# A bidirectional mLSTM and neighbourhood-attention layer: state products for both directions as three split products of 258 columns

## The chip, the cores and the metric

The kernel runs on one core of a Trainium2 chip. The metric is device time in microseconds (us) of one execution. TensorE appears in the profile as PE (its weight loads as PEld), VectorE as DVE, ScalarE as ACT, GpSimd as POOL; SP is the sync engine, which issues most of the DMAs. The queues by which an engine issues DMAs are shown as SPq, ACTq, POOLq.

## The reference, cut to what matters

One layer over 2048 tokens of 1024 features, all float32. After a conditioned RMSNorm one projection gives the inputs of two groups: neighbourhood attention (8 heads of 64 on a grid 32 x 64) and a bidirectional mLSTM (4 heads of 128). q and k of the mLSTM go through a convolution of 5 taps and SiLU. The outputs of both groups are gated, joined, projected and added to x, and a final RMSNorm follows. The part that the change touches is the state recurrence of the mLSTM, run forwards and backwards:

```python
def step(carry, inp):
    C, n, m = carry
    ...
    w = jnp.exp(a_c - m_new[..., None])
    C_new = decay[..., None, None] * C + jnp.einsum('bhs,bhse,bhsd->bhed', w, v_c, k_c)
    n_new = decay[..., None] * n + jnp.einsum('bhs,bhsd->bhd', w, k_c)
```

The kernel works in chunks of 128 tokens (NC = 16 chunks, MH = 4 heads) and holds C and n of a head in one tile of 128 x 129 by giving v a column of ones: the state's addition in a chunk is the product of k (128 tokens x 128 features) with v (128 tokens x 129) scaled by the row weights w of that direction.

## The kernel before, in words

**Projections.** The large products are split: an operand x becomes a high part, rounded to float32r by ACT, and a low part, x minus high, by DVE, and a product is hi*hi + hi*lo + lo*hi on TensorE. The token blocks (`tok_blocks`) and the convolution (`conv_blocks`) come first. In the convolution each group of 512 tokens of one feature tile is projected (24 products of 512 columns), evicted by ACT, run through five taps on DVE (L1032, L1034) and SiLU on ACT (L1036), and stored in `d_ck`, a scratch tensor in device memory that holds for each head and chunk everything that the mLSTM reads. For k, TensorE also turns the four chunks of the group (L1045), ACT copies them out with the scale KSCALE (L1047) and SP stores them as 128 columns of `d_ck`, in front of v.

**The mLSTM.** `phase1b` takes the heads in turn, each in two passes. `ml_pass1` goes through the 16 chunks from both ends to the middle (0, 15, 1, 14, ...). `load` (SP queue, seven buffers) brings k and v of a chunk, 257 columns; `weight` scales v for the directions that need it (DVE, L1263: direction 1 into a tile of its own, `wv`, four buffers, direction 0 in place); a step makes one float32 product per direction (L1283), and the state of the next chunk is either updated from the one before (`follow`, DVE, L1267) or put aside by an ACT copy (L1294), to be joined later: at the end of the pass DVE runs 14 further `follow`s. In the first two steps of a head (chunks 0 and 15) one direction has no next chunk and gets no product. `ml_pass2` then computes the outputs chunk by chunk; its first product with a state is px (L1344).

**Fillers.** Between the steps `pump` puts products of `nq_gen` (L1094: the projections of attention's q and k and of the gates, 24 products of 512 columns per tile) on TensorE, PUMP1 = 4.5 per step of the first pass. For each weight column pair the fillers need a split too: an ACT copy to high (L1065, L1067) and a DVE subtraction to low (L1066, L1068); their results are evicted by ACT and DVE.

**Order.** Up to attention a planner of the framework orders each engine's instructions by its own costs and by readiness, so that an instruction may come well ahead of its place in the text. The attention part of `phase2` runs in `manual_schedule`, in the order as written. Attention's softmax works on a ring of ten tiles of 128 x 512. Since the transposes read some columns past the used ones, all ten are cleared to zero before, by GpSimd (L1748), just ahead of the hand-ordered part. The first slot of that part makes two pairs of scores (L1587, four PSUM banks), with the softmax of the first pair (L1598 on DVE, L1599 on ACT) between.

Of the kernel before, what the change touches and what calls it, by code (L numbers as in the profile page):

```python
# [8 lines left out]
F32 = mybir.dt.float32  # L9
F32R = mybir.dt.float32r  # L10
AF = mybir.ActivationFunctionType
ALU = mybir.AluOpType
# [3 lines left out]
P = 128  # L16
# [9 lines left out]
MH = 4  # L26
# [32 lines left out]
class Kernel:  # L59
# [30 lines left out]
    def scratch(self):  # L90
        d = self.dram
        self.d_vna = d.tile([T, 512], F32, name="d_vna")
        self.d_ck = d.tile([MH, NC, P, 897], F32, name="d_ck")
        self.d_mneg = d.tile([P, CH], F32, name="d_mneg")
        self.d_zna = d.tile([16, P, 4, P], F32, name="d_zna")
        self.d_zml = d.tile([16, P, 4, P], F32, name="d_zml")
        self.d_qna = d.tile([2, 16, P, 2, 2, P], F32, name="d_qna")
        self.d_kna = d.tile([2, 512, T], F32, name="d_kna")
        self.d_mix = d.tile([16, P, 4, P], F32, name="d_mix")
        self.d_wo = d.tile([KT, P, D], F32, name="d_wo")  # L100
        self.d_fnw = d.tile([1, D], F32, name="d_fnw")
        self.d_gate = d.tile([1, D], F32, name="d_gate")
        self.d_rneg = d.tile([NH, 15, 31], F32, name="d_rneg")
        nks = [24, 32, 24]
        self.d_e = [d.tile([NH // 2, 16, 2, 15, nks[t]], F32, name=f"d_e{t}") for t in range(3)]
        nrs = [11, 15, 12]
        self.d_t = [[d.tile([NH // 2, P, 2, nrs[r] * nks[t]], F32, name=f"d_t{r}{t}") for t in range(3)] for r in range(3)]
# [588 lines left out]
    def vo_group(self, h, slot, g, first=None, brow=None, tops=(), stage=None):  # L696
        nc = self.nc
        st = self.stage_tile(f"stvo_{h}_{g}") if stage is None else stage
        nc.gpsimd.memset(st[:, :, 128:129], 1.0)
        brow = brow if brow is not None else self.brows[h % 2]  # L700
        width = 272 if h == 0 else 256
        for o in range(4):
            tt = 4 * g + o
            if first:
                ps = first[o]
            else:
                ps = tops[o] if o < len(tops) else self.pp.tile([P, GT], F32, tag="pp", name=f"pvo_{h}_{tt}")
                self.tok_tile(ps[:, :width], self.wslot[slot], tt, width)
            pair = st[:, o].rearrange("p (j c) -> p j c", j=2)[:, :, 0:128]
            self.evicted = nc.vector.tensor_add(pair, ps[:, 0:256].rearrange("p (j c) -> p j c", j=2), brow.rearrange("p (j c) -> p j c", j=2))  # L710
            if h == 0:
                nc.vector.tensor_add(self.gates[:, :, tt], ps[:, 256:272], self.bgate)
            next(self.chain, None)
            if o == 1:
                self.flush()
        nc.scalar.activation(st[:, :, 129:257], st[:, :, 129:257], AF.Sigmoid)
        dst = self.d_ck[h, 4 * g : 4 * g + 4, :, 128:385].rearrange("o p c -> p o c")
        if g == 0 and h < 3:
            (nc.scalar if h == 0 else nc.sync).dma_start(dst, st[:, :, 0:257])
        else:  # L720
            self.defer(lambda: nc.sync.dma_start(dst, st[:, :, 0:257]))
# [186 lines left out]
    def decays(self, pool):  # L908

        nc = self.nc  # L910
        mask = pool.tile([P, 2, CH], F32, name="mask")
        nc.gpsimd.memset(mask, 0.0)
        nc.gpsimd.affine_select(out=mask[:, 0, :], in_=mask[:, 0, :], pattern=[[1, CH]], compare_op=ALU.is_ge, fill=-BIG, base=0, channel_multiplier=-1)
        nc.gpsimd.affine_select(out=mask[:, 1, :], in_=mask[:, 1, :], pattern=[[-1, CH]], compare_op=ALU.is_ge, fill=-BIG, base=0, channel_multiplier=1)
        groups = [(h, gi, d) for h in range(MH) for gi in range(NG) for d in range(2)]
        tiles = {}

        def load(n):
            h, gi, d = groups[n]
            t = tiles[n] = self.dec_tile(pool, f"dec_{n}")  # L920
            r = d * 64 + h * NC + 4 * gi
            src = self.d_mneg[r : r + 4].rearrange("r t -> (r t)").unsqueeze(0)
            self.behind(nc.sync.dma_start(t, src.broadcast_to([P, 512])), self.mark)

        def masked(n):
            t = tiles[n].rearrange("p (c t) -> p c t", c=4)
            nc.gpsimd.tensor_tensor(t, t, mask[:, groups[n][2]].unsqueeze(1).broadcast_to([P, 4, CH]), ALU.add)  # L927

        def raised(n):
            h, gi, d = groups[n]  # L930
            t = tiles.pop(n).rearrange("p (c t) -> p c t", c=4)
            for o in range(4):
                c = 4 * gi + o
                nc.scalar.activation(t[:, o, :], t[:, o, :], AF.Exp, bias=self.cols["g"][:, d, h, c : c + 1])  # L934
            dst = self.d_ck[h, 4 * gi : 4 * gi + 4, :, 641 + d * CH : 641 + (d + 1) * CH].rearrange("c p t -> p c t")
            nc.scalar.dma_start(dst, t)

        for n in range(len(groups) + 3):
            for step, fn in ((3, raised), (2, masked), (0, load)):
                if 0 <= n - step < len(groups):  # L940
                    fn(n - step)
            yield
# [80 lines left out]
    def conv_group(self, pool, u, kind, ct, g):  # L1023
# [11 lines left out]
        yield  # L1035
        nc.scalar.activation(acc, acc, AF.Silu, bias=self.cb[:, cc : cc + 1])  # L1036
        j = 0 if kind == "q" else 1
        dst = self.d_ck[ct, 4 * g : 4 * g + 4, :, 385 + j * CH : 385 + (j + 1) * CH].rearrange("c p t -> p c t")
        nc.sync.dma_start(dst, acc.rearrange("p (c t) -> p c t", t=CH))
        yield  # L1040
        if kind == "q":
# [1 line left out]
        ps = self.tp.tile([P, GT], F32, tag="tp", name=f"kt_{ct}_{g}")  # L1043
        for o in range(4):
            nc.tensor.transpose(ps[:, o * P : (o + 1) * P], acc[:, o * CH : (o + 1) * CH], self.ident)  # L1045
        st = self.stage_tile(f"stk_{ct}_{g}")[:, :, 0:128]
        nc.scalar.activation(st, ps.rearrange("p (a q) -> p a q", a=4), AF.Copy, scale=KSCALE)  # L1047
        d2 = self.d_ck[ct, 4 * g : 4 * g + 4, :, 0:128].rearrange("o p c -> p o c")
        nc.sync.dma_start(d2, st)


    def nq_load(self, i, s):
# [193 lines left out]
    def ml_pass1(self, ml, h):  # L1246
# [3 lines left out]
        order = [k // 2 if k % 2 == 0 else NC - 1 - k // 2 for k in range(NC)]  # L1250

        def load(k):
            t = tiles[k] = ml.tile([P, 257], F32, tag="kv", bufs=7, name=f"kv_{h}_{order[k]}")
            nc.sync.dma_start(t, self.d_ck[h, order[k], :, 0:257])

        def weight(k):
            c = order[k]
            v = tiles[k][:, 128:257]
            sides[k] = {d: v for d in range(2) if 0 <= c + 1 - 2 * d < NC}
            if len(sides[k]) == 2:  # L1260
                sides[k][1] = ml.tile([P, 129], F32, tag="wv", bufs=4, name=f"wv_{h}_{c}")
            for d in sorted(sides[k], reverse=True):
                nc.vector.tensor_scalar(sides[k][d], v, self.cols["w"][:, d, h, c : c + 1], None, ALU.mult)  # L1263

        def follow(d, c, dc):
            n = c + 1 - 2 * d
# [8 lines left out]
        for k, c in enumerate(order):  # L1275
            if k + 4 < NC:
                load(k + 4)
            self.flush(2)
            self.close_step()
            dc = self.ms.tile([P, 2, 256], F32, tag="s1", bufs=3, name=f"dc_{h}_{c}")  # L1280
            kt = tiles.pop(k)[:, 0:128]
            for d, w in sorted(sides[k].items()):
                nc.tensor.matmul(dc[:, d, :129], kt, w, start=True, stop=True)  # L1283
            if k + 2 < NC:
                weight(k + 2)
            for d in sorted(sides.pop(k)):
                n = c + 1 - 2 * d
                self.st[d][n] = ml.tile([P, 129], F32, tag=f"st{d}_{n}", name=f"st_{h}_{d}_{n}")
                if k < 2:
                    nc.vector.tensor_copy(self.st[d][n], dc[:, d, :129])  # L1290
                elif d == k % 2:
                    follow(d, c, dc[:, d, :129])
                else:
                    nc.scalar.activation(self.st[d][n], dc[:, d, :129], AF.Copy)  # L1294
            self.low()
            self.pump(PUMP1)
            yield
# [9 lines left out]
    def ml_pass2(self, ml, h):  # L1307
# [3 lines left out]

        def load(c):
            t = ml.tile([P, 769], F32, tag="ck", bufs=4, name=f"ck_{h}_{c}")
            nc.sync.dma_start(t, self.d_ck[h, c, :, 128:897])
            vo[c] = t[:, 0:257]
            qk[c] = t[:, 257:513].rearrange("p (j t) -> p j t", j=2)
            mb[c] = t[:, 513:769].rearrange("p (d t) -> p d t", d=2)
# [143 lines left out]
    def phase2(self):  # L1461
# [282 lines left out]
        pO = self.pool(pss, "pO", bufs=1, space=PSUM)  # L1744
        ring = [few.tile([P, 512], F32, tag=tag, bufs=bufs, name=f"ring_{i}") for i, (tag, bufs) in enumerate((("hm", 2), ("hm", 2), ("zt", 2), ("zt", 2)))]
        ring += [p.tile([P, 512], F32, name=f"ring_{i}") for i in range(4, 10)]
        for t in ring[4:] + ring[:4]:
            nc.gpsimd.memset(t, 0.0)  # L1748
        order = itertools.cycle(ring)
        turn = lambda: next(order)  # L1750
        b1 = patches[1]
# [113 lines left out]
                self.owed = 0  # L1865

        with self.tc.manual_schedule():
            for m in range(len(patches) + 1):
                slot(m)
            while len(done) < len(patches):  # L1870
# [94 lines left out]
```

## Time and profile before

| | us |
|---|---|
| median of 3 runs | 1277.48 (1276.66 to 1277.92) |
| profiled execution, its own time | 1276.39 |
| its span | 1274.5 |
| PE busy | 1264.4 (99%) |
| DVE busy | 790.3 (62%) |
| ACT busy | 537.7 (42%) |
| POOL busy | 201.7 (16%) |

The span is from the first to the last instruction of the profiled execution. Times within it are in us from its start. The granted TensorE clock was at full speed (0.999 on the mean). Matmuls overlap: one that lasts 0.4 us may be followed 0.23 us later by the next, so busy PE says nothing of how dense its work is. The convolution lies from about 310 to 490 us, the four heads from 533 to 905 us, attention and the output from 915 us on.

### The profile page before, as it was taken

What the parts mean: (1) busy time and instruction counts of PE and PEld (TensorE: products, weight loads), DVE (VectorE), ACT (ScalarE), POOL (GpSimd) and SP (SyncE); (2) the same over time, 40 slices, a digit from 0 to 9 for tenths busy, and PEclk for the clock granted to TensorE, in tenths of its full rate; (3) what the DMA queues carried; (4) which work ended last, traced back from release to release, by engine and by line L of the source; (5) the groups of instructions that cost most, each with busy time, mean ns of one, the idle gap of its engine ahead of it and who ended that gap; (6) DMA issues with size and microseconds to landing.
All of it is one profiled execution on the core that took longest, in us unless ns stands there. A gap on an engine that the chain in (4) does not pass through costs nothing.

```text
span 1274.5 us, 22948 instructions
## 1 busy us (share of the span) xinstructions
PE 1264.4 (99%) x8168; PEld 1095.4 (86%) x8168; DVE 790.3 (62%) x2391; ACT 537.7 (42%) x1182; POOL 201.7 (16%) x368
## 2 busy tenths in 40 slices
PE   9999999999999999999999999999999999999997
PEld 8999999999888888888888888888877888888886
DVE  7875542213667664267777778777556766767664
ACT  6642425442334222123323323324357565565552
POOL 0000003440000000000001001000424331332541
PEclk9999999999999999999999999999999999999999
DMA  9999947996678764745757867746677755655551
GB/s 366 335 309 286 283 147 198 249 245 180 180 180 189 165 154 115 207 131 164 204 160 207 251 189 215 240 149 186 207 249 266 230 162 160 203 177 176 176 173 67
DMA packets 217082, 259.08 MB, mean 203 GB/s; under 512 B 23435, under 2 KB 163595, under 8 KB 216968
## 3 DMA queue, kind: packets, MB, share of 16 engines
q1 hardware_dynamic: 149542, 190.09, 52.1%
q0 software_dynamic: 13616, 37.28, 8.9%
q10 hardware_dynamic: 53810, 30.24, 8.4%
q8 instruction: 65, 1.06, 0.3%
q14 instruction: 49, 0.40, 0.1%
HBM read 173.05 MB, written 92.72 MB: 209 GB/s over the span
## 4 chain that ended last, share of the span: by engine, by line
PE 95%; DVE 2%; ACT 1%; issue 1%; DMA 0%; DVEq 0%; ACTq 0%
PE pq L1094 27%; PE y L1676 14%; PE pc L639 5%; PE pc L640 5%; PE pc L638 5%; PE pO L1633 4%; PE pT L1618 3%; PE pvo L638 3%; PE pvo L640 3%; PE pvo L639 3%; PE pS L1587 3%; PE pvo L693 3%; PE pv L640 2%; PE pv L639 2%; PE pv L638 2%; PE pi L1346 2%
## 5 line engine op out<-in xcount | busy, mean ns | idle before, releaser
L1094 PE MATMUL pq<-hhi,whi_a 128*128 128x512 f32 x512 | 208.4, 407 | 0.0
L1094 PE MATMUL pq<-hlo,whi_a 128*128 128x512 f32 x512 | 207.8, 406 | 0.0
L1094 PE MATMUL pq<-hhi,wlo_a 128*128 128x512 f32 x512 | 207.2, 405 | 0.0
L1368 POOL TENSOR_TENSOR hm<-hm,ck 128x128 f32<-128x128 f32 x64 | 28.2, 440 | 580.3 <-DVE hm L1367 541.0
L1094 PEld LDWEIGHTS pq<-hhi,wlo_a 128*128 128x128 f32 x512 | 96.8, 189 | 16.7 <-issue 0.2
L1094 PEld LDWEIGHTS pq<-hlo,whi_a 128*128 128x128 f32 x512 | 96.7, 189 | 16.1 <-issue 0.4
L1094 PEld LDWEIGHTS pq<-hhi,whi_a 128*128 128x128 f32 x512 | 96.8, 189 | 15.9
L1599 ACT ACTIVATE ring<-ring,mn 128x480 f32<-128x480 f32 (+5 forms) x128 | 75.9, 594 | 55.8 <-DVE mn L1598 55.8
L1620 ACT ACTIVATE ring<-pT 96x384 f32<-96x384 f32 (+3 forms) x128 | 65.8, 514 | 63.5 <-PE pT L1618 62.0
L1676 PE MATMUL y<-hhi,wlo_a 128*128 128x512 f32 (+1 forms) x272 | 87.0, 394 | 0.2 <-ACT y L1683 0.2
L1676 PE MATMUL y<-hhi,whi_a 128*128 128x512 f32 x256 | 86.2, 408 | 0.0
L1349 ACT ACTIVATE num<-px,gtile 128x129 f32<-128x129 f32 x120 | 38.7, 367 | 105.2 <-PE px L1344 91.5
L1522 POOL DMA_DIRECT2D v<-d_vna x158 | 78.7, 505 | 15.6 <-issue 4.4
L1618 PEld LDWEIGHTS pT<-ident,ring 128*128 128x128 f32 (+2 forms) x416 | 51.1, 136 | 19.2 <-ACT ring L1620 3.7
L1618 PE MATMUL pT<-ident,ring 128*128 128x128 f32 (+2 forms) x416 | 66.2, 272 | 0.0
L638 PE MATMUL pvo<-whi_b,hhi 128*128 128x256 f32 x224 | 63.6, 284 | 0.0
L1598 DVE CUSTOM_DVE_ANT_0 ring<-pS,tab 128x480 f32<-128x480 f32 (+5 forms) x128 | 61.9, 539 | 2.6 <-PE pS L1587 2.4
L640 PE MATMUL pvo<-whi_b,hlo 128*128 128x256 f32 x224 | 63.1, 282 | 0.0
L639 PE MATMUL pvo<-wlo_b,hhi 128*128 128x256 f32 x224 | 63.0, 281 | 0.0
L934 ACT ACTIVATE dec<-dec,gtile 128x128 f32<-128x128 f32 x128 | 41.3, 391 | 46.9 <-POOL dec L927 43.2
L673 DVE TENSOR_TENSOR stv<-pv,brow 128x256 f32<-128x256 f32 x32 | 13.6, 425 | 71.8 <-PE pv L640 71.8
L710 DVE TENSOR_TENSOR stvo<-pvo,brow 128x256 f32<-128x256 f32 x60 | 24.7, 418 | 50.7 <-PE pvo L640 40.0
(343 smaller groups left out, 3331.3 us busy)
## 6 DMA issues: line engine op xcount, KB each, us to landing
ck<-d_ck SPq DMA_DIRECT2D x64, 384.5 KB, 3.6
rawq<-in_w_main_dram SPq DMA_DIRECT2D x28, 512.0 KB, 5.2
raw<-in_w_main_dram SPq DMA_DIRECT2D x18, 512.0 KB, 6.2
kv<-d_ck SPq DMA_DIRECT2D x64, 128.5 KB, 3.0
dec<-d_mneg SPq DMA_DIRECT2D x32, 256.0 KB, 6.0
d_ck<-dec ACTq DMA_DIRECT2D x32, 256.0 KB, 6.9
qs<-d_qna SPq DMA_DIRECT2D x30, 256.0 KB, 3.9
xr<-in_x_p_dram POOLq DMA_DIRECT2D x15, 512.0 KB, 3.9
```

Of the source, the lines that this page charges most:

```text
L638: nc.tensor.matmul(ps, lhi(k), rhi(k), start=(k == 0), stop=False)
L639: nc.tensor.matmul(ps, lhi(k), rlo(k), start=False, stop=False)
L640: self.mark = nc.tensor.matmul(ps, llo(k), rhi(k), start=False, stop=(k == KT - 1))
L934: nc.scalar.activation(t[:, o, :], t[:, o, :], AF.Exp, bias=self.cols["g"][:, d, h, c : c + 1])
L1094: self.mark = nc.tensor.matmul(patch_ps(ps) if patch else ps, w, self.htok(h, g, k, patch), start=(k == 0 and n == 0), stop=(k == KT - 1 a ...
L1522: queue.dma_start(chunks[key][r * nkc : (r + 1) * nkc, :], rows[r])
L1598: nc.vector.tensor_tensor_reduce(pt[:, :nk], ps, tabs[ct][:, j * nk : (j + 1) * nk], 1.0, 3e38, ALU.add, ALU.min, mn)
L1599: nc.scalar.activation(pt[:, :nk], pt[:, :nk], AF.Exp, bias=mn, scale=-1.0, accum_out=sums[:, j : j + 1])
L1618: nc.tensor.transpose(ps[:cs, i, :], U[u][j][:, i * cs : (i + 1) * cs], self.ident)
L1620: nc.scalar.activation(t[:cs, :nch, :], ps[:cs, :nch, :], AF.Copy)
L1633: nc.tensor.matmul(po[j * HD : (j + 1) * HD, ct, :], v[:n, h * HD : (h + 1) * HD], pt[j][:n, i, :], start=(i == 0), stop=(i == nch - 1))
L1676: nc.tensor.matmul(y, m[:, k, :], w[k][:, cs], start=(k == 4 and n == 0), stop=(k == 3 and n == 2))
```

## The change

- In the convolution the turned k leaves as two parts: ACT writes the high part (rounded to float32r), DVE the rest, `KSCALE * k - high` (scalar_tensor_tensor from PSUM). Both are stored, so k takes 256 instead of 128 columns of `d_ck`, whose rows grow from 897 to 1025 columns; every other column range moves by 128.
- In the first pass the kv tile is 385 columns. `weight` splits v times w for both directions of every chunk, the two directions side by side: ACT makes the high parts (two activations), DVE the low parts (two scalar_tensor_tensor that read the high parts), into tiles w0 and w1 of 2 x 129 columns with three buffers each. A step makes three products of 258 columns into one PSUM bank, k-high with w-high, k-high with w-low, k-low with w-high, in the end chunks too, where one of the directions is not used.
- The clearing of the ring goes from GpSimd to DVE, covers columns 256 to 511 alone, and stands at the beginning of the hand-ordered part.

```diff
     def conv_group(self, pool, u, kind, ct, g):
...
-        st = self.stage_tile(f"stk_{ct}_{g}")[:, :, 0:128]
-        nc.scalar.activation(st, ps.rearrange("p (a q) -> p a q", a=4), AF.Copy, scale=KSCALE)
-        d2 = self.d_ck[ct, 4 * g : 4 * g + 4, :, 0:128].rearrange("o p c -> p o c")
-        nc.sync.dma_start(d2, st)
+        st = self.stage_tile(f"stk_{ct}_{g}")
+        hi, lo = (st[:, :, e * P : (e + 1) * P] for e in range(2))
+        turned = ps.rearrange("p (a q) -> p a q", a=4)
+        nc.scalar.activation(hi.bitcast(F32R), turned, AF.Copy, scale=KSCALE)
+        nc.vector.scalar_tensor_tensor(lo.bitcast(F32R), turned, KSCALE, hi, ALU.mult, ALU.subtract)
+        d2 = self.d_ck[ct, 4 * g : 4 * g + 4, :, 0:256].rearrange("o p c -> p o c")
+        nc.sync.dma_start(d2, st[:, :, 0:256])
     def ml_pass1(self, ml, h):
...
         def weight(k):
             c = order[k]
-            v = tiles[k][:, 128:257]
-            sides[k] = {d: v for d in range(2) if 0 <= c + 1 - 2 * d < NC}
-            if len(sides[k]) == 2:
-                sides[k][1] = ml.tile([P, 129], F32, tag="wv", bufs=4, name=f"wv_{h}_{c}")
-            for d in sorted(sides[k], reverse=True):
-                nc.vector.tensor_scalar(sides[k][d], v, self.cols["w"][:, d, h, c : c + 1], None, ALU.mult)
+            v = tiles[k][:, 256:385]
+            hi, lo = sides[k] = [ml.tile([P, 2, 129], F32R, tag=f"w{e}", bufs=3, name=f"w{e}_{h}_{c}") for e in range(2)]
+            for d in range(2):
+                w = self.cols["w"][:, d, h, c : c + 1]
+                nc.scalar.activation(hi[:, d, :], v, AF.Copy, scale=w)
+                nc.vector.scalar_tensor_tensor(lo[:, d, :], v, w, hi[:, d, :].bitcast(F32), ALU.mult, ALU.subtract)
...
-            for d, w in sorted(sides[k].items()):
-                nc.tensor.matmul(dc[:, d, :129], kt, w, start=True, stop=True)
+            khi, klo = (tiles[k][:, e * P : (e + 1) * P].bitcast(F32R) for e in range(2))
+            tiles.pop(k)
+            whi, wlo = sides.pop(k)
+            for n, (a, b) in enumerate(((khi, whi), (khi, wlo), (klo, whi))):
+                nc.tensor.matmul(dc, a, b, start=n == 0, stop=n == 2)
...
     def phase2(self):
...
-        for t in ring[4:] + ring[:4]:
-            nc.gpsimd.memset(t, 0.0)
...
         with self.tc.manual_schedule():
+            for t in ring:
+                nc.vector.memset(t[:, 256:], 0.0)
             for m in range(len(patches) + 1):
                 slot(m)
```

## Rows read from the trace of the kernel before

**Rows 1.** The page, part 1: busy us, share of the span, instructions.
```profile
PE 1264.4 (99%) x8168; PEld 1095.4 (86%) x8168; DVE 790.3 (62%) x2391; ACT 537.7 (42%) x1182; POOL 201.7 (16%) x368
```
**Rows 2.** Waits of PE: who waited for whom, us in total, times, longest.
```profile
PE pvo L436 <- ACT hhi L404: 1.2, 2, 0.8
PE dense L348 <- DVE eps L116: 1.1, 1, 1.1
...
```
**Rows 3.** Table by stretches: start:end, length, busy us of each engine, clock, DMA.
```profile
core 0: us, PE busy (x) PEld busy (x) DVE busy (x) ACT busy (x) POOL busy (x), PEclk, DMA share, GB/s
330.00:420.00 90.00, 90.00 (x420) 73.27 (x419) 60.59 (x121) 31.42 (x49) 0.00 (x0) 1.00 0.78 182
533.00:560.00 27.00, 27.00 (x151) 23.25 (x151) 17.25 (x60) 6.84 (x19) 0.00 (x0) 1.00 0.48 131
```
**Rows 4.** The chain that ended last, in order of time: start, us, what.
```profile
82.94 12.09 PE pvo L693 x96
...
491.53 41.70 PE pq L1094 x180
```
**Rows 5.** The line of the first pass's products: count, ns min/median/max, first and last start.
```profile
L1283 PE MATMUL dc<-kv x128: 271/273/276, 533.1 to 834.1; 128*128 128x129 f32 x128
L1283 PE MATMUL dc<-wv,kv x112: 275/275/276, 535.8 to 834.3; 128*128 128x129 f32 x112
```
**Rows 6.** Timeline of PE in head 0's first pass: start, us, what.
```profile
536.97 0.38 PE L1283 MATMUL dc<-kv 128*128 128x129 f32 x2
...
548.89 0.38 PE L1283 MATMUL dc<-kv 128*128 128x129 f32 x2
```
**Rows 7.** Timeline of PE in the token blocks, products of 256 columns.
```profile
149.74 0.28 PE L639 MATMUL pvo<-wlo_a,hhi 128*128 128x256 f32 x1
...
152.93 0.28 PE L639 MATMUL pvo<-wlo_a,hhi 128*128 128x256 f32 x1
```
**Rows 8.** Groups by line and shape, DVE and ACT: busy us, mean ns; idle before.
```profile
L1267 DVE SCALAR_TENSOR_TENSOR st<-st,gtile,dc 128x129 f32<-128x129 f32 x56 | 18.9, 346 | 11.2 <-PE dc L1283 9.1 <-ACT st L1294 1.8
L1263 DVE TENSOR_SCALAR kv<-kv,gtile 128x129 f32<-128x129 f32 x64 | 17.6, 285 | 21.0 <-DMA kv<-d_ck 19.9
L1294 ACT ACTIVATE st<-dc 128x129 f32<-128x129 f32 x56 | 15.4, 278 | 47.2 <-DVE st L1267 34.7 <-PE dc L1283 10.4 <-DVE wv L1263 1.7
```
**Rows 9.** Timeline of DVE and PEld where first passes end: head 1, then head 2.
```profile
648.15 0.48 DVE L1263 TENSOR_SCALAR wv<-kv,gtile 128x129 f32<-128x129 f32 x2
...
651.64 1.66 DVE L1267 SCALAR_TENSOR_TENSOR st<-st,gtile,st 128x129 f32<-128x129 f32 x6
653.63 0.42 PEld L1344 LDWEIGHTS px<-st,ck 128*128 128x128 f32 x2
...
746.92 0.30 PEld L1344 LDWEIGHTS px<-st,ck 128*128 128x128 f32 x2 [0.45 <-DVE st L1267]
```
**Rows 10.** Groups by line and shape, DVE, 330 to 513 us: the convolution's taps.
```profile
L1034 DVE SCALAR_TENSOR_TENSOR acc_k<-u,cw,acc_k 128x512 f32<-128x512 f32 x54 | 37.9, 747 | 0.5
```
**Rows 11.** DMA issues (KB, us to landing), and waits of SP's queue, 510 to 840.
```profile
kv<-d_ck SPq DMA_DIRECT2D x64, 128.5 KB, 3.0
...
SPq L1254 <- PE dc L1283: 42.5, 39, 6.9
```
**Rows 12.** Memsets of DVE by shape, then timelines of DVE and PEld ahead of attention.
```profile
L999 DVE MEMSET u<- 128x2 f32 x8 | 0.5, 60 | 0.0
L114 DVE MEMSET ones<- 128x128 f32 x1 | 0.2, 165 | 0.8 <-PEq L1952 0.8
...
925.02 0.75 DVE L1137 SCALAR_TENSOR_TENSOR qst<-pq,bcol,qst 128x512 fp32r<-128x512 f32 x1 [3.59 <-ACT qst L1136]
927.96 0.46 DVE L1598 CUSTOM_DVE_ANT_0 ring<-pS,tab 128x288 f32<-128x288 f32 x1 [2.18 <-PE pS L1587]
...
929.28 0.43 PEld L1587 LDWEIGHTS pS<-hhi,qs 64*128 64x128 f32 x6 [0.37 <-DVE mn L1598]
```
**Rows 13.** Timelines of ACT and PE early in head 1's first pass.
```profile
628.84 1.06 ACT L1065 ACTIVATE whi_a<-rawq 128x1024 fp32r<-128x1024 f32 x1 [5.11 <-PE pq L1094]
629.34 0.38 PE L1283 MATMUL dc<-kv 128*128 128x129 f32 x2
```

More of the change, by code (lines that the diff above doesn't have):

```diff
@@ L92, in scratch @@
         self.d_vna = d.tile([T, 512], F32, name="d_vna")
-        self.d_ck = d.tile([MH, NC, P, 897], F32, name="d_ck")
+        self.d_ck = d.tile([MH, NC, P, 1025], F32, name="d_ck")
         self.d_mneg = d.tile([P, CH], F32, name="d_mneg")
@@ L716, in vo_group @@
         nc.scalar.activation(st[:, :, 129:257], st[:, :, 129:257], AF.Sigmoid)
-        dst = self.d_ck[h, 4 * g : 4 * g + 4, :, 128:385].rearrange("o p c -> p o c")
+        dst = self.d_ck[h, 4 * g : 4 * g + 4, :, 256:513].rearrange("o p c -> p o c")
         if g == 0 and h < 3:
@@ L934, in raised @@
                 nc.scalar.activation(t[:, o, :], t[:, o, :], AF.Exp, bias=self.cols["g"][:, d, h, c : c + 1])
-            dst = self.d_ck[h, 4 * gi : 4 * gi + 4, :, 641 + d * CH : 641 + (d + 1) * CH].rearrange("c p t -> p c t")
+            dst = self.d_ck[h, 4 * gi : 4 * gi + 4, :, 769 + d * CH : 769 + (d + 1) * CH].rearrange("c p t -> p c t")
             nc.scalar.dma_start(dst, t)
@@ L1037, in conv_group @@
         j = 0 if kind == "q" else 1
-        dst = self.d_ck[ct, 4 * g : 4 * g + 4, :, 385 + j * CH : 385 + (j + 1) * CH].rearrange("c p t -> p c t")
+        dst = self.d_ck[ct, 4 * g : 4 * g + 4, :, 513 + j * CH : 513 + (j + 1) * CH].rearrange("c p t -> p c t")
         nc.sync.dma_start(dst, acc.rearrange("p (c t) -> p c t", t=CH))
@@ L1252, in load @@
         def load(k):
-            t = tiles[k] = ml.tile([P, 257], F32, tag="kv", bufs=7, name=f"kv_{h}_{order[k]}")
-            nc.sync.dma_start(t, self.d_ck[h, order[k], :, 0:257])
+            t = tiles[k] = ml.tile([P, 385], F32, tag="kv", bufs=7, name=f"kv_{h}_{order[k]}")
+            nc.sync.dma_start(t, self.d_ck[h, order[k], :, 0:385])
         def weight(k):
             c = order[k]
-            v = tiles[k][:, 128:257]
-            sides[k] = {d: v for d in range(2) if 0 <= c + 1 - 2 * d < NC}
-            if len(sides[k]) == 2:
-                sides[k][1] = ml.tile([P, 129], F32, tag="wv", bufs=4, name=f"wv_{h}_{c}")
-            for d in sorted(sides[k], reverse=True):
-                nc.vector.tensor_scalar(sides[k][d], v, self.cols["w"][:, d, h, c : c + 1], None, ALU.mult)
+            v = tiles[k][:, 256:385]
[4 more added lines that the diff above has]
+                nc.vector.scalar_tensor_tensor(lo[:, d, :], v, w, hi[:, d, :].bitcast(F32), ALU.mult, ALU.subtract)
         def follow(d, c, dc):
@@ L1279, in ml_pass1 @@
             self.close_step()
-            dc = self.ms.tile([P, 2, 256], F32, tag="s1", bufs=3, name=f"dc_{h}_{c}")
-            kt = tiles.pop(k)[:, 0:128]
-            for d, w in sorted(sides[k].items()):
-                nc.tensor.matmul(dc[:, d, :129], kt, w, start=True, stop=True)
+            dc = self.ms.tile([P, 2, 256], F32, tag="s1", bufs=3, name=f"dc_{h}_{c}").rearrange("p a b -> p (a b)")[:, :258].rearrange("p (d c) -> p d c", d=2)
+            khi, klo = (tiles[k][:, e * P : (e + 1) * P].bitcast(F32R) for e in range(2))
[3 more added lines that the diff above has]
+                nc.tensor.matmul(dc, a, b, start=n == 0, stop=n == 2)
             if k + 2 < NC:
                 weight(k + 2)
-            for d in sorted(sides.pop(k)):
+            for d in range(2):
                 n = c + 1 - 2 * d
+                if not 0 <= n < NC:
+                    continue
                 self.st[d][n] = ml.tile([P, 129], F32, tag=f"st{d}_{n}", name=f"st_{h}_{d}_{n}")
                 if k < 2:
-                    nc.vector.tensor_copy(self.st[d][n], dc[:, d, :129])
+                    nc.vector.tensor_copy(self.st[d][n], dc[:, d, :])
                 elif d == k % 2:
-                    follow(d, c, dc[:, d, :129])
+                    follow(d, c, dc[:, d, :])
                 else:
-                    nc.scalar.activation(self.st[d][n], dc[:, d, :129], AF.Copy)
+                    nc.scalar.activation(self.st[d][n], dc[:, d, :], AF.Copy)
             self.low()
@@ L1313, in load @@
             t = ml.tile([P, 769], F32, tag="ck", bufs=4, name=f"ck_{h}_{c}")
-            nc.sync.dma_start(t, self.d_ck[h, c, :, 128:897])
+            nc.sync.dma_start(t, self.d_ck[h, c, :, 256:1025])
             vo[c] = t[:, 0:257]
```

## The prediction, made before the change was run

> **What bounds the kernel now.** I read the page's first part first: TensorE (PE) is busy 99% of the 1274.5 us, VectorE (DVE) 62%, ScalarE (ACT) 42% [rows 1]. Then the waits of PE: five kinds, 3.1 us in all, 2.3 of them (the two shown) at the start of the program [rows 2]. Then a table by stretches: in those that the change touches PE is busy throughout, while DVE is busy for 67% (convolution) and 64% (first pass of head 0) [rows 3]. So but for the first 60 us and the tail the time is the sum of the start-to-start distances of PE's instructions, and these, not the durations, are PE's prices: 180 fillers of 512 columns take 41.70 us, 0.2317 each [rows 4]. The profiled execution took 1276.39 us, 1.89 over its span; the median of the runs is 1277.48, 1.09 more. I make the sum against the profiled execution and carry the difference to the median.
>
> **Products of the first pass (PE).** 64 chunks x 2 directions less 8 end pieces are 120 float32 products, and the trace has 240 instructions for them, two per product [rows 5]. From the dc at 536.97 to that at 548.89 lie 8 steps with 36 fillers (4.5 per step): 11.92 - 36 x 0.2317 = 3.58, so a step's two float32 products cost 0.4475 us, one 0.224 [rows 6]. After, a step is three float32r products of 258 columns. Their neighbours in the trace: 96 of 272 columns take 12.09 us, 0.1259 each [rows 4], and from 149.74 to 152.93 lie 27 distances of 256 columns, 0.118 each [rows 7]. Interpolated, 258 columns cost 0.119, three 0.357; both neighbours change the stationary operand each time too, so its load hides. 56 steps with both directions: 56 x (0.4475 - 0.357) = 5.07 us less. The 8 end chunks had one product and get the same three: 8 x (0.357 - 0.224) = 1.06 more. Net -4.0 us. Bounds: by 272 columns (three 0.378) -3.89 + 1.23 = -2.7; by 256 columns (three 0.354) -4.2. I take the interpolation, as 258 is next to 256.
>
> The Trainium skill ("TensorE: Matmul & The Clock Gate", section "Back-to-back issue gap") gives a warm distance of N/2.4 + 2.5 ns, 110 ns at 258 columns; by it three would cost 0.330 and the term would be -5.7 us. It says 109 where the 256-column rows show 118 [rows 7], so the measured distance decides.
>
> **Weights of the products.** Before, DVE makes one scaled copy per direction, 120 of 0.285 us. After, per chunk ACT makes two high parts (nearest row: a 128x129 copy, 0.278) and DVE two remainders (nearest: a 128x129 scalar_tensor_tensor, 0.346) [rows 8]. A step of PE becomes 4.5 x 0.2317 + 0.357 = 1.40 us; DVE then has three such instructions, 1.04, and a share of the fillers' splits and evictions, about 0.25: 1.29, it still fits. ACT goes from 25% (6.84 of 27 [rows 3]) to some 65%. The lead is two steps in the text and three chunks by buffers, 2.8 to 4.2 us, against 2 x 0.28 + 2 x 0.35 = 1.3: 0 in steady state. Without that cover each hold of ACT costs PE directly (the slower rival).
>
> **The end of each pass.** Here the trace is tight. After the last dc DVE runs 14 state updates, one after the other, before PE's first px of the second pass. In head 1 DVE first makes four scaled copies for the next head (two pairs from 648.15, the first shown), 0.8 us; the chain's last piece ends at 653.30 and px's weights load at 653.63: 0.3 us spare. In head 2 PE waits 0.45 us for the chain [rows 9]. Heads 0 and 3 have 0.7 by the same two rows. The four copies become four remainders, 0.3 instead of 0.2 each at the rows' spacing, so the chain is 0.4 later; and the ACT copy of the last state may stand behind two high parts (0.56). Added stalls with +0.4: 0, 0.1, 0.4, 0; with +1.0: 0.3, 0.7, 1.0, 0.3. Bounds -0.45 (the chain put first, head 2's wait gone) and 2.3; I take 0.7, near the first case, since the copies stood ahead of the chain in the rows.
>
> **k split in the convolution.** ACT's copy per k group stays; DVE gets one scalar_tensor_tensor of 128x512 for each of 16 groups, nearest row 0.747 [rows 10]: 12 us in a stretch of 90, DVE goes from 67% to 81%. PE waits for DVE nowhere there [rows 2, 3]: 0. The store doubles to 512 KB and waits for DVE instead of ACT, and what is behind it on SP's queue (weight blocks, table copies, output weights) is issued up to about 1 us later; the blocks are asked for four groups, 20 us, ahead: 0, and if that cover went, tenths for each of four blocks. The added 4.2 MB are 47 GB/s on 182 at a DMA share of 0.78 [rows 3], near full, one reason for the upper end. The kv loads grow from 128.5 to 192.5 KB; they land in 3.0 us, and SP mostly waits for a buffer that a dc frees, so they run up to seven chunks ahead [rows 11]: 0. The pitch and the offsets of d_ck: 0.
>
> **Ring clearing.** Ten GpSimd memsets go; what GpSimd waits for next is a DMA, so 0. Ten DVE memsets of 128x256 come into the hand-ordered part ahead of the first softmax. DVE took 0.165 for 128x128 and 0.060 for 128x2, so 256 columns are about 0.27, ten 2.7 us. They start when the eviction begun at 925.02 ends, 925.77, and end at 928.5; the first softmax instruction started at 927.96, so it comes 0.5 late. PE's second scores at 929.28 need the four score banks back and were already released by DVE [rows 12]; the last of the four, begun 1.1 after the first, has some 0.15 to spare. Cost 0.4; bounds 0 (they slip into DVE's idle time before 925.02) and 1.0 (0.33 each, twice the 128-column row).
>
> For the memset the Trainium skill ("VectorE: DVE Perf Modes", section "Zero memsets can be issued as uint32 (trn2)") says one cycle per element whatever the dtype: 0.267 us for 256 at its 0.96 GHz, without a fixed part. By it the ten end at 928.4 and the cost is 0.3. DVE's two memset rows agree with that rate [rows 12]; no run here shows 256 columns.
>
> **Sum.** -4.0 + 0.7 + 0.4 = -2.9 us: 1273.5 for the profiled execution, 1274.6 for the median (-0.23%). About 0.2%, 2.55 us, is what a measurement of this kernel can tell from no change.
>
> **Rivals.**
> 1. *The saving is eaten at the seams.* The chain at the pass ends is 1.0 late instead of 0.4 (2.3 us) and the memsets cost 1.0: -4.0 + 3.3 = -0.7, 1276.8. For it: head 2 already waits, and DVE works on the chain without a gap [rows 9]. Against: heads 0 and 3 have 0.7 us spare.
> 2. *Slower: high parts stuck on ACT.* ACT runs in order and serves the filler too: at 628.84 it started a weight split (1.06) after waiting 5.11 us for PE to release the buffer, while a dc ran at 629.34 [rows 13]. If a chunk's high parts stand behind such a split, they end at 628.84 + 1.06 + 0.56 = 630.46, the remainder at 630.8, and PE waits 1.5 us. A split falls on every second filler tile (48 products), a pass has 81 fillers, so the four passes have about seven; five hits are 7.5 us: 1277.48 - 2.9 + 7.5 = 1282.1. It decides when a hold of ACT exceeds the lead of about 2.8 us. For it: nothing urgent hung on ACT in this pass before. Against: the planner puts ready work first, and a chunk's high parts are ready when the buffer of three chunks before is released.
> 3. *Nothing is lost at the seams*: the planner orders the chain ahead of the next head's weights, the memsets slip into DVE's earlier idle time. -4.0 to -4.4 (the 0.45 wait goes as well): 1273.3.
>
> **How the numbers follow.** Forecast (1273.6 to 1275.6) 50%, rival 1 25%, rival 2 13%, rival 3 12%. The limit for faster is 1274.92: two thirds of the forecast and all of rival 3, 0.33 + 0.12 = 0.45; slower is rival 2, 0.13; the rest 0.42. The range runs from 1272.9 (rival 3 with the -4.2 bound and the scatter of the runs) to 1278.3 (rival 1 and one hit of rival 2, or tenths from DMA in the convolution); what it leaves out is most of rival 2 and little else.
>
> **What would show it.** Right: dc 192 instructions; a pass-1 step of 1.40 us instead of 1.49 on PE with nothing between; a pass of 16 steps 1.0 us shorter; PE's px waits of 0 to 0.5 per head on DVE st; the first softmax instruction about 0.5 later relative to the first scores; no PE wait in the convolution. Wrong: 258 columns costing clearly over 0.126 each, PE waits on the weight parts or on ACT inside the pass, or kt transposes that wait for DVE.

## The result, and the profile after

The changed kernel takes 1282.05 us (median of 10 runs, 1278.82 to 1285.35), the kernel before 1277.28 beside it (10 runs): ratio 1.0037, 95% interval 1.0026 to 1.0048. It is 4.8 us slower by the medians, where 1274.6 was forecast and the range ended at 1278.3.

The profiled execution of the changed kernel took 1285.35 us, the longest of its runs; its span is 1283.6, 9.1 over that of before, so the trace shows the loss about twice as large as the median. Part of that is the clock: its mean grant was 0.994 in this run, the lowest of the ten, and 0.999 in the shortest (1278.82). Its page, parts 1 and 2 (busy time and share of the span per engine; the granted clock by slices):

```profile
span 1283.6 us, 23103 instructions
...
PE 1266.4 (99%) x8120; PEld 1096.5 (85%) x8120; DVE 809.7 (63%) x2425; ACT 574.8 (45%) x1310; POOL 197.8 (15%) x358
...
PEclk9998999999999999999999999999999999999999
```

PE's share hardly differs from [rows 1], so the share says nothing of where 9 us went. The starts of four landmarks do (us, from the traces; e1 and e2 are experiments told below: the changed kernel and the kernel before, each with another row length of `d_ck`):

| first start of | before | after | e1 | e2 |
|---|---|---|---|---|
| convolution (pc at L639) | 306.2 | 314.4 | 306.6 | 312.7 |
| the 180 fillers ahead of the first pass | 491.53 | 503.59 | 491.93 | 501.91 |
| attention's first scores (pS) | 927.16 | 936.21 | 924.63 | 937.8 |

Up to the convolution the changed kernel loses 8.2 us and in it 3.9 more (503.59 - 314.4 against 491.53 - 306.2): 12.1, all ahead of the mLSTM. Through the four heads it gains 3.0 (432.62 against 435.63 from the second landmark to the third), and from the first scores to the end both take 347.3. So the products gained, and the loss lies where the prediction had put nothing. The rows of the second and third landmark, from the chain and from PE's timeline of the changed kernel (start, us, instruction):

```profile
503.59 41.70 PE pq L1097 x180
...
936.21 0.67 PE L1594 MATMUL pS<-hhi,qs 64*128 64x288 f32 x6
```

PE's waits of the changed kernel (us in total, times, longest), the answer to [rows 2]:

```profile
PE pvo L693 <- DVE stvo L710: 2.5, 2, 2.0
PE kt L1045 <- ACT acc_k L1036: 2.2, 1, 2.2
PE pc L638 <- DVE stv L673: 1.6, 1, 1.6
PE dense L348 <- DVE eps L116: 1.1, 1, 1.1
PE pvo L436 <- ACT hhi L404: 0.8, 1, 0.8
PE ht L1407 <- ACT hm L1400: 0.8, 1, 0.8
```

The first three are new, 6.3 us, and all three lie ahead of the mLSTM. In two of them PE waits for DVE. What DVE itself waits for between 60 and 340 us:

```profile
DVE stv L673 <- DMA d_vna<-stv: 33.7, 4, 9.6
DVE stvo L710 <- DMA d_ck<-stvo: 8.2, 2, 5.5
...
DVE stv L673 <- DMA d_ck<-stvo: 4.2, 1, 4.2
```

Before, DVE waits for neither store in this stretch. L710 writes the next block of v into a stage buffer, and the buffer is free when the store of an earlier block has landed. The largest of these waits is for stores of `d_vna`, whose rows the change left alone; they use the same stage buffers and the same queue (SPq) as those of `d_ck`. The chain of the changed kernel from 80 us shows the first of these waits becoming the path:

```profile
81.54 23.14 DMA d_ck<-stvo x2
...
105.14 0.41 DVE stvo L710
105.56 0.67 DVE h L411
...
106.25 0.74 ACT hhi L412
...
110.87 0.43 DVE stvo L710
```

Two stores of `d_ck`, 23.14 us with what they waited for, then DVE's eviction, then the splits behind it on DVE in order; PE stops twice, for 2.5 us in all. In the same stretch before, the chain is PE alone, `PE pvo L693 x96` in 12.09 us [rows 4]. After the stall the granted clock falls for a while. Windows (us, busy time and instructions of PE, PEld, DVE, ACT and POOL, granted clock, DMA share, GB/s), two of after and one of before:

```profile
110.00:160.00 50.00, 48.66 (x380) 48.25 (x381) 22.58 (x55) 15.62 (x21) 1.28 (x7) 0.93 1.03 255
110.70:117.50 6.80, 6.16 (x27) 6.16 (x28) 6.53 (x11) 3.29 (x5) 0.11 (x1) 0.50 1.08 342
```

```profile
110.00:160.00 50.00, 50.00 (x417) 49.45 (x416) 25.77 (x72) 17.49 (x22) 1.27 (x7) 1.00 1.00 274
```

380 products instead of 417 in the same 50 us: 37 at 0.118 to 0.126 [rows 4, 7] are 4.4 to 4.7 us. PE is idle for 1.34 of them; the other 3.4 are 6.8 us at half the clock. The wait for kt does the same in the convolution. There the chain runs through the output weights (`wraw`) that DVE scales between the taps:

```profile
355.35 4.77 DMA d_wo<-wraw
...
360.18 3.96 DMA wraw<-in_w_out_dram
...
365.39 0.60 DVE stk L1050
365.99 2.00 DVE acc_k L1034 x3
...
368.01 0.73 ACT acc_k L1036
...
368.79 0.66 PE kt L1045 x4
369.44 0.23 PE pc L638
...
370.46 0.43 PE pc L639
```

PE waits 2.2 us for kt. The first products behind it are 0.23 apart, as before the stall; from 370.46 they are 0.43 apart: the 1.2 GHz level instead of 2.4. The window says the same:

```profile
370.10:373.50 3.40, 3.40 (x10) 2.64 (x9) 2.85 (x6) 0.64 (x2) 0.00 (x0) 0.50 0.47 127
```

3.4 us at half the clock cost 1.7, and with the wait of 2.2 that is the 3.9 lost in the convolution. So the 12.1 us ahead of the mLSTM are the three waits (6.3), the two stretches at the lower clock (3.4 and 1.7), and 0.5 that was lost before the token blocks, whose first product at L638 starts at 46.40 instead of 45.91: 11.9.

What is different about the stores is their landing time. DMA issues (count, KB each, median us from issue to landing), after and before:

```profile
d_ck<-dec ACTq DMA_DIRECT2D x32, 256.0 KB, 8.2
...
d_ck<-stvo SPq DMA_DIRECT2D x14, 514.0 KB, 7.0
...
d_ck<-acc_k SPq DMA_DIRECT2D x16, 256.0 KB, 6.3
```

```profile
d_ck<-dec ACTq DMA_DIRECT2D x32, 256.0 KB, 6.9
...
d_ck<-stvo SPq DMA_DIRECT2D x14, 514.0 KB, 5.3
...
d_ck<-acc_k SPq DMA_DIRECT2D x16, 256.0 KB, 5.0
```

These three store what they stored before, same bytes and same engine. Only the place differs: a row of `d_ck` has 1025 columns, 4100 bytes, instead of 897, 3588 bytes.

### The profile page after: what moved, and what is told of

It reads as the page before. It is cut to its first block, busy times and chain, and to the rows that moved or that the text cites. A ratio compares the mean times of both kernels' runs of the same rounds, so it can differ in the third digit from the quotient of the medians.

```text
span 1283.6 us, 23103 instructions
## 1 busy us (share of the span) xinstructions
PE 1266.4 (99%) x8120; PEld 1096.5 (85%) x8120; DVE 809.7 (63%) x2425; ACT 574.8 (45%) x1310; POOL 197.8 (15%) x358
## 4 chain that ended last, share of the span: by engine, by line
PE 77%; DMA 16%; DVE 3%; ACT 2%; issue 1%; POOL 1%; SPq 0%; ACTq 0%; DVEq 0%; POOLq 0%
PE pq L1097 27%; PE y L1683 14%; PE pO L1640 4%; PE pc L639 3%; PE pc L640 3%; PE pc L638 3%; PE pT L1625 3%; DMA dec<-d_mneg 3%; DMA d_ck<-dec 3%; PE pS L1594 3%; PE pi L1353 2%; PE pvo L638 2%; PE pvo L640 2%; PE px L1351 2%; PE pvo L639 2%; DMA d_ck<-stvo 2%
## 5 line engine op out<-in xcount | busy, mean ns | idle before, releaser
L638 PE MATMUL pvo<-whi_b,hhi 128*128 128x256 f32 x224 | 63.6, 284 | 0.0
L639 PE MATMUL pvo<-wlo_b,hhi 128*128 128x256 f32 x224 | 63.0, 281 | 0.0
L710 DVE TENSOR_TENSOR stvo<-pvo,brow 128x256 f32<-128x256 f32 x60 | 24.7, 419 | 57.6 <-PE pvo L640 39.3
```

The source lines that it names most:

```text
L638: nc.tensor.matmul(ps, lhi(k), rhi(k), start=(k == 0), stop=False)
L639: nc.tensor.matmul(ps, lhi(k), rlo(k), start=False, stop=False)
```

## Experiments

Theories at the start: **P**, a row length next to 4096 bytes slows the stores; **L**, any longer row does; **K**, it is not the row but the doubled store of k and DVE's added work. All comparisons are with the kernel before on the same chip.

**e1: the changed kernel with longer rows.**

```diff
-        self.d_ck = d.tile([MH, NC, P, 1025], F32, name="d_ck")
+        self.d_ck = d.tile([MH, NC, P, 1153], F32, name="d_ck")
```

> The changed kernel with d_ck's rows padded from 1025 to 1153 columns (4100 to 4612 bytes), nothing else. Theory P (rows whose pitch is next to 4096 bytes make every store into d_ck slow): the stores come back to the times of before (the 514 KB one from 7.0 to about 5.3 us), the 6.3 us lost ahead of the value blocks and most of the 3.8 lost in the convolution go, the 3 us gained in the heads stay: 1273 to 1275. Theory L (any longer row is slow): 1282 or more, stores 7 us or more. Theory K (the doubled k store and DVE's new work cost it): about 1282, stores as in the changed kernel.

1274.05 us, ratio 0.9975 (0.9965 to 0.9985): faster than both, by 3.1 us than before, and by 8.0 us than the changed kernel, by one number in the code (the medians of the kernel before were 1277.28 and 1277.17 beside the two). Its PE waits, in part:

```profile
PE pvo L436 <- ACT hhi L404: 1.2, 2, 0.8
...
PE ht L1407 <- ACT hm L1400: 0.8, 1, 0.8
```

None of the three new waits is left; the 514 KB store lands in 5.4 us. From pc at L639 to the fillers e1 takes 185.33 us, as before does, with all of the k split in it. K falls.

**e2: the kernel before with the changed kernel's row; e3: with e1's.** 897 becomes 1025 (e2) and 1153 (e3), nothing else.

> The kernel before with d_ck's rows of 1025 instead of 897 columns, columns at their old places, nothing else. Theory P: the stores slow to about 7 us, DVE waits for them near 100 us, 6 to 10 us lost: 1284 to 1287. Theory L: the same. Theory K: 1277, nothing changes, as k is not split.

> The kernel before with rows of 1153 columns (4612 bytes). Theory P: 1277, as before. Theory L (longer rows are slower): at least as slow as rows of 1025, 1284 or more. Theory K: 1277.

e2: 1285.69, ratio 1.0064 (1.0049 to 1.0078), +8.5 us by the medians, 8.2 by the ratio, with not one product changed. e3: 1277.14, 0.9998 (0.9989 to 1.0006). So the row alone is the whole loss, and length alone is not it: L falls. e2's store rows and the waits that PE did not have before:

```profile
d_ck<-stvo SPq DMA_DIRECT2D x14, 514.0 KB, 7.6
```

```profile
PE kt L1045 <- ACT acc_k L1036: 3.2, 3, 2.6
PE pvo L693 <- DVE stvo L710: 2.8, 2, 2.0
PE pv L638 <- DVE stv L673: 1.2, 1, 1.2
```

**e4: exactly 4096 bytes.** 897 becomes 1024.

> The kernel before with rows of 1024 columns, exactly 4096 bytes. Theory P: at least as slow as 1025 columns, 1284 or more, 514 KB stores of 7 us or more. If only a row start that is not a multiple of 64 bytes matters, it is faster than 1025 columns and 1277 or less, since here every row starts on one. Theory K: 1277.

1277.02, ratio 0.9993 (0.9985 to 1.0002); the store lands in 5.5 us. P in its plain form falls: at 4096 itself nothing is lost.

**e5, e6, e7: which distance from 4096.** The changed kernel with 1040 columns (4160 bytes); the kernel before with 1021 (4084) and with 2049 (8196, 4 bytes over twice 4096).

> The changed kernel with rows of 1040 columns: 4160 bytes, a multiple of 64, still next to 4096. The runs so far: rows of 1025 columns are slow, of 897, 1024 and 1153 are not. Theory N (a row start off the 64-byte grid and a pitch next to a multiple of 4096 bytes, both together, make the stores slow): 1273 to 1275, 514 KB stores about 5.4 us. Theory A (near 4096 but not 4096 itself is enough): 1282 or more, stores of 7 us.

> The kernel before with rows of 1021 columns: 4084 bytes, 12 below 4096 and off the 64-byte grid. Theory N and theory A: stores of 7 us, 1283 or more. If only the exact pitch of 4100 bytes (or one just above 4096) is slow: 1277.

> The kernel before with rows of 2049 columns: 8196 bytes, 4 over twice 4096. Theory N: as rows of 1025, stores of 7 us, 1283 or more. If it takes neighbouring rows at 4 KB, not the same place in every 4 KB: 1277.

e5: 1274.39, 0.9972 (0.9962 to 0.9983), as e1. e6: 1291.05, 1.0102 (1.0085 to 1.0119), the worst of all. e7: 1288.97, 1.008 (1.0067 to 1.0092). So it is a few bytes beside a multiple of 4096, on either side and for either multiple. DVE's waits for the stores in e6 and e7:

```profile
DVE stv L673 <- DMA d_ck<-stvo: 10.3, 2, 5.4
DVE stvo L710 <- DMA d_ck<-stvo: 7.5, 2, 5.0
```

```profile
DVE stvo L710 <- DMA d_ck<-stvo: 5.6, 1, 5.6
DVE stv L673 <- DMA d_ck<-stvo: 5.6, 1, 5.6
```

In e7 the median landing of that store is only 5.8 us, near the 5.3 of before, and yet DVE waits 5.6 for one of them: the median of all 14 can hide the few that decide. The packets of the traces tell the slow rows apart where the medians don't: 8192 packets of 1028 bytes carry the stores of v in every run, and their mean is 58.8 ns in the changed kernel, 63.6 in e2, 63.2 in e6 and 58.9 in e7, but 51.3 to 54.4 in the kernel before and in all other runs of this document; 5.6 to 9.2% of them take over 100 ns, against 0.7 to 2.4%. So these stores are slow on their way, and not only late in the queue. The packets of 1024 bytes from 215 to 340 us, nearly all of them of the `d_vna` stores in the kernel before, show no such order (52.8 ns in e6, 63.7 in e4, which loses nothing): those stores wait with the others and are not shown to be slow themselves.

**e8: the ring.** e1 with the ring cleared whole by GpSimd, as before, instead of in half by DVE.

```diff
+        for t in ring[4:] + ring[:4]:
+            nc.gpsimd.memset(t, 0.0)
...
-            for t in ring:
-                nc.vector.memset(t[:, 256:], 0.0)
```

> The changed kernel with rows of 1153 columns and the ring cleared by GpSimd, whole tiles, as before. The prediction had the DVE memsets at 0.4 us: then this is 1273.6. In the trace of the changed kernel they lie in idle time of DVE ten us before the first softmax: then there is no difference, 1274.0, both within 0.5.

1274.38, 0.9972 (0.9962 to 0.9983), against e1's 0.9975: no difference that these times can tell. Their intervals are some 1.3 us wide to either side, so the 0.4 that was forecast for the ring could hide in them; the rows below decide.

**e9 to e11: alignment, nearness or drift.** Theories now: **N**, rows that start off a 64-byte grid and lie near such a multiple; **A**, nearness within some tens of bytes is enough; **D**, the place of a row modulo 4096 moves by only a few bytes from one row to the next. e9 is e4 with every column range of `d_ck` moved by one column, so that the pieces of k and v start 4 bytes off the grid, and the others 8, without drift; e10 is 1033 columns (36 bytes over), e11 1089 (260 over).

```diff
-        dst = self.d_ck[h, 4 * g : 4 * g + 4, :, 128:385].rearrange("o p c -> p o c")
+        dst = self.d_ck[h, 4 * g : 4 * g + 4, :, 129:386].rearrange("o p c -> p o c")
```

> The kernel before with rows of 1024 columns (4096 bytes), every column range moved by one column, so that v's and k's rows start 4 bytes off the 64-byte grid, all at the same place in their 4 KB. Theory N (off the grid and near a multiple of 4096 bytes): stores of 7 us, 1283 or more. Theory D (it takes rows whose place in 4 KB drifts by a few bytes from row to row, as with 1021, 1025 and 2049 columns, and not a start off the grid): 1277, stores of 5.5 us.

> The kernel before with rows of 1033 columns: 4132 bytes, 36 over 4096, off the grid. If being near to 4096 within one 64-byte line decides: slow, 1283 or more. If only drifts of a few bytes (4 to 12) are slow: 1277 to 1279.

> The kernel before with rows of 1089 columns: 4356 bytes, 260 over 4096, off the grid. By theories N and D it is far enough from 4096: 1277 to 1278, 514 KB stores of about 5.4 us. If the slow stretch around 4096 is wide, some hundred bytes: 1280 or more.

e9: 1277.88, 1.0 (0.9991 to 1.0008). e10: 1278.43, 1.0004 (0.9996 to 1.0013). e11: 1276.82, 0.9995 (0.9986 to 1.0004). None is slow. N falls with e9 (off the grid, at 4096), A with e10 as far as 36 bytes; D stands, as a description and not as a mechanism.

**e12: 16 bytes over.** 1028 columns, 4112 bytes.

> The kernel before with rows of 1028 columns: 4112 bytes, a drift of 16 over 4096; 12 was slow and 36 was not. Theory D gives no number for it. If the loss shrinks steadily with the drift: about 1281, halfway. If it stops between 12 and 16: 1277.

1277.85, 1.0004 (0.9995 to 1.0013). The kernel loses nothing, but the stores are not quite free: the 514 KB store takes 6.2 us and DVE waits for stores without PE noticing.

```profile
DVE stv L673 <- DMA d_vna<-stv: 16.3, 4, 5.0
...
DVE u L999 <- DMA d_ck<-dec: 2.0, 1, 2.0
```

The rows tried, as bytes from a multiple of 4096, and what each cost its kernel: -12 (+13 us), +4 (+8.5, and +11 at 8196) slow; 0, +16, +36, +260, +516 within 1.2 us of before; +64 and +516 in the changed kernel 3.1 to 3.3 us faster than before. Above a multiple the loss ends, or falls below what the buffers cover, between 4 and 16 bytes; below it only 12 was tried. A longer row also moves whatever lies behind `d_ck` in memory; no run moves that alone. What the memory does in these cases no trace shows, only packet and landing times and the waits behind them. That the waits for a stage buffer are the only way from a late store to PE was read from the chains; a kernel with more stage buffers was not tried.

## Why the prediction was wrong

**The step that failed** is the last sentence on the k split in the convolution: "The pitch and the offsets of d_ck: 0". It was given no bounds and no rival of its own. Undone alone (e1) it returns 8.0 us, done alone (e2) it costs 8.5; with 3.1 of gain from the rest, 8.0 - 3.1 = 4.9 is the measured 4.8. The prediction weighed the bytes that the change adds to the convolution, but the stores that became late first, of v at 81.54, carry the bytes that they always did. Before, DVE waited for none of them. The prediction named the cover and its price for the weight blocks, and not for these stores. One of its signs did tell: it named "no PE wait in the convolution", and PE waits 2.2 us there.

**Products, forecast -4.0: right in mechanism, a little short in size.** The 192 instructions are there, three per step. PE's timeline of e1 in head 0:

```profile
541.90 0.53 PE L1288 MATMUL dc<-w,kv 128*128 128x258 f32 x3
...
547.53 0.52 PE L1288 MATMUL dc<-w,kv 128*128 128x258 f32 x3
```

From 541.90 to 547.53 lie four steps with 18 fillers: 5.63 - 18 x 0.2317 = 1.46, 0.365 a step; over head 0's 15 distances the mean is 0.361, against 0.357 forecast. At 0.361 the term is 56 x (0.4475 - 0.361) - 8 x (0.361 - 0.224) = 3.75 us of gain.

**Pass ends, forecast +0.7: right in size by luck, wrong in place.** The chain of follows is not late: the wait for px that head 2 had before, 0.45 [rows 9], is gone in the changed kernel and in e1. Instead ACT holds PE once inside the first pass of head 3, in e1 and in the changed kernel alike. PE and ACT of e1:

```profile
816.15 0.52 PE L1288 MATMUL dc<-w,kv 128*128 128x258 f32 x3
...
817.44 0.33 PE L1407 MATMUL ht<-ident,hm 128*128 128x128 f32 x1 [0.77 <-ACT hm L1400]
...
818.92 0.53 PE L1288 MATMUL dc<-w,kv 128*128 128x258 f32 x3
```

```profile
816.31 0.70 ACT L1265 ACTIVATE w<-kv,gtile 128x129 fp32r<-128x129 f32 x2 [1.15 <-DMA kv<-d_ck]
816.91 0.86 ACT L1400 ACTIVATE hm<-hm,mu,rstd 128x128 f32<-128x128 f32 x2
```

ACT, in order, waits 1.15 us for a kv load, makes the two high parts, and only then the normalised output that PE is to turn. The step takes 2.77 us with five fillers and two ht; 2.77 - 5 x 0.2317 = 1.61, where the same step in heads 1 and 2 of e1 leaves 0.58 and 0.57. That is 1.0 us. The first steps of heads 1 to 3 also leave 0.44 to 0.46 instead of 0.36, 0.3 in all. So the seams cost 1.0 + 0.3 - 0.45 = 0.85, and -3.75 + 0.85 = -2.9, against -3.0 measured from landmark to landmark. The kv loads, priced at 0 because they run ahead, stand by ACT's row at the root of 1.0; no run takes that wait away alone.

**Weights: the durations were low, the verdict held.** The scaled ACT copy takes 395 ns, not the 278 of the nearest row, and DVE's remainder 352, near the 346 assumed [rows 8]. Durations (min, median, max) in the changed kernel:

```profile
L1265 ACT ACTIVATE w<-kv,gtile x128: 387/395/408, 538.6 to 840.1; 128x129 fp32r<-128x129 f32 x128
```

In steady state PE waits for neither.

**The k split itself, forecast 0: right**, by e1's 185.33 us. DVE's remainder takes 0.685 there, under the 0.747 taken as its bound.

**Ring, forecast +0.4: 0.** DVE of the changed kernel:

```profile
925.23 2.46 DVE L1874 MEMSET ring<- 128x256 f32 x9
...
936.92 0.46 DVE L1605 CUSTOM_DVE_ANT_0 ring<-pS,tab 128x288 f32<-128x288 f32 x1 [2.09 <-PE pS L1594]
```

Nine take 2.46, 0.273 each, as forecast; but they run some 9 us ahead of the first softmax instruction, which then waits for PE. They took the lower bound's way, into DVE's idle time. The prediction's sentence that DVE's two memset rows agree with the rate cited there does not come out of them: from 2 to 128 columns they rise by (0.165 - 0.060) / 126 = 0.83 ns a column, and 0.267 for 256 would be 1.04. The measured 0.273 lies near both all the same.

**The rivals.** Without the row length the kernel lands between the forecast and rival 3: 1277.28 - 3.1 = 1274.2. Rival 2 named 1282.1, almost the measured time, but for a reason that did not happen: it wanted five holds of 1.5 us of PE by weight splits on ACT in the first pass, and there is one hold of 0.8, from a kv load. That its time fits is luck; the place of the loss, ahead of the first pass, told the two apart.

## What to carry to other kernels

When an edit changes the shape of a scratch tensor in device memory, its row length is a change of its own: the place of every store and load to it moves, also of those that the edit doesn't touch, so bound that cost from the waits that each store's buffer has to spare. If a kernel gets slower at an edit that should gain, look first where the landmarks separate, then at the landing times of transfers whose bytes are the same. And where PE's clock falls behind a wait, as it did twice here, the wait costs more than its own length.

## What the runs showed of the hardware

The 514 KB stores into `d_ck` (4 x 128 rows, 1028 bytes written in each, 14 of them per run) landed in 7.0 to 7.6 us, by the median, at a row length of 4100 bytes and in 8.0 at 4084, where 3588, 4096, 4160, 4356 and 4612 bytes took 5.1 to 5.5. Between lie 4112 bytes with 6.2 and 4132 with 5.8, without loss, and 8196 with 5.8 and a loss of 11 us; the packets of these stores part them (58.8 to 63.6 ns on the mean in the kernels that lost, 51.3 to 54.4 in the others). At exactly 4096 nothing was lost.

The Trainium skill ("DMA: Bandwidth & Descriptors", section "Latency and other measured facts") tells of copies that slow down where the row pitch is a large power of two, at 2 MiB and above, while 512 KiB is not slow, and where padding by 192 bytes doesn't help and by 4 KiB does. No run here has such a pitch, so none bears on it. What these runs add is a loss at short rows that are no power of two, 4100, 4084 and 8196 bytes (1285.69, 1291.05, 1288.97), and none at 4096, which is one (1277.02).

Two waits of PE of 2.5 us together, around 110 us, were followed by 6.8 us at a granted clock of 0.50, which cost 3.4 us, more than the waits did; one of 2.2 us in the convolution was followed by 3.4 us at 0.50. It is not so after every wait: in e2 PE waits up to 2.6 us for kt, and the window from 380 to 430 us, which holds that wait, shows a granted clock of 1.00.
